# The down projection of a one-core encoder layer: a new order of its work, of its queues and of its sums

## The chip, the cores and the metric

The kernel runs on one core of one Trainium2 chip, as one launch. The metric is the device time of that launch in microseconds (us), and less is better. The core has five engines with a program each: TensorE (PE in the profile, its weight loads PEld), VectorE (DVE), ScalarE (ACT), GpSimd (POOL) and SyncE (SP), which only starts transfers. Sixteen DMA engines move data between the device's memory (DRAM) and the core's on-chip memory (SBUF). Transfers started by SP go through the hardware queue, those started by GpSimd through the software queue. TensorE writes its products to PSUM, a small memory of banks that VectorE and ScalarE read.

## What is computed

One layer of an encoder trunk, for 512 prompt frames and 64 frames of a running stream, in fp32. The change lies in its last part, the SwiGLU feed-forward block; x is the residual stream ahead of it.

```python
def rmsnorm(x, g):
    return x * lax.rsqrt(jnp.mean(x * x, axis=-1, keepdims=True) + EPS) * g

# ahead of this: norm, one input projection, stick-breaking attention on 8 heads, a gated short
# convolution on 8 channel groups, norm, output projection, residual
h2 = rmsnorm(x, g_norm2)                                        # (576, 2048)
x = x + (jax.nn.silu(h2 @ w_gate) * (h2 @ w_up)) @ w_down       # 2048 -> 5632 -> 2048
```

## The kernel before, in words

**Layout.** All activations are held transposed: 128 channels on the partitions, frames along the free axis, the 576 frames in two halves of 288 (`HALVES`). The hidden width of 5632 is 22 pairs (`NFP`) of 128-channel blocks; the 2048 output channels are 8 output blocks (`DC`) of two 128-channel columns each.

**fp32 by three products.** A weight or a frame tile is split into a rounded high part and the rest (`split`, L216: a ScalarE cast at L217, a VectorE subtraction at L218). A product is then three matmuls of 128x128 by 128x288: high by high, low by high, high by low. `multiply` (L1065) issues them; their line in the profile is L1069.

**Seven products per unit.** The feed-forward block is computed by a scheme in the manner of Strassen and Winograd. The two columns of weights and the two halves of the hidden pair and of the frames make 2x2 blocks, and seven products p = 1 to 7 take the place of eight. They need sums of weight blocks (L1055 to L1059, on VectorE: `s1`, `a21`, `a11`, and `a12` for p = 3) and sums of frame blocks, called forms: seven of them, each in a high and a low part. A unit is one entry of the list `UNITS`: 42 gate and up units, one per hidden pair 1 to 21 and per matrix (pair 0 is done ahead by `wide`, L972), and then the down visits. The products of neighbouring units are interleaved: (n+1,1), (n,3), (n,4), (n+1,2), (n+1,6), (n+1,7), (n+1,5). `prepare` (L1045) makes the sums and splits the weights of a product `AHEAD` = 2 products before `run` (L1073) multiplies. Accumulators in PSUM are shared between products: `psy` collects products 1, 6, 5 and 3 of a unit, `psw` products 7 and 4; ScalarE copies a state of `psy` that is needed later to SBUF (`kept`, L1079; tile `part`, one buffer per tag).

**Down visits.** The table `DOWN` (L44) has one entry (block, first pair, last pair) per visit: a visit multiplies the frames of its m pairs by that block's weights. There are 36 visits with m from 3 to 7. All 8 blocks must have gone past a pair before its storage is free for another (`down_calls`, L53).

**Frames.** At the end of gate and up, `put_form` (L922) stores each form to `hid_dram` from GpSimd's queue, 288 KB each. `load_pair` (L1148) reads one pair, seven forms in both parts, back as one load of 2016 KB from GpSimd's queue (L1152) into one of `SLOTS` = 7 slots. Pairs 0 to 2 are loaded during the last up unit, into storage of the activations `h2`; 3 at the first down visit, 4 to 6 at the next three, into storage of the frame sums (`tsum`, L896); the others when a slot comes free (L1217 on).

**Weights.** `load_weight` (L177, issue at L180) loads one 128-channel column of a unit from SP's queue, one load per column, two units ahead, into a buffer of 8 KB per partition, of which there are four.

**Residual and output.** `load_x2` (L1124) reads the residual x (`x2_dram`, written at L867) in 144 KB pieces from GpSimd's queue, 4 per block, and `add` (L1144) adds each result of a visit to it on VectorE, 7 additions a visit: four from PSUM, three from `part`. After the last visit of a block, `store_y` (L1154) waits three ticks (a tick is issued behind every pair of a product), transposes each 128x288 result on TensorE (L1173), copies it to a single output buffer `ob` on VectorE and ScalarE (L1174, L1176), and stores it from GpSimd's queue (L1163 to L1178).

**What sets the order.** TensorE's program is in the order in which the code is written, by hand, throughout (`manual_schedule`, L110). The other engines' programs are ordered by the language's own scheduler, except in an early stage (L360). Every DMA that SP starts takes one of eight lanes in turn and waits until the transfer eight before it on its queue is done.

## Time and profile before

| | us |
|---|---|
| median of the three runs | 2516.56 (2516.19 to 2518.26) |
| profiled execution, its own time | 2514.56 |
| span of that execution | 2512.9 |
| TensorE busy | 2427.3 (97%) |
| VectorE busy | 1759.8 (70%) |
| ScalarE busy | 1073.3 (43%) |
| GpSimd busy | 284.8 (11%) |
| mean granted TensorE clock | 0.988 of full speed |
| traffic | 269.33 MB read, 64.31 MB written |

The page of the profile gives busy time per engine, the span in 40 slices, DMA queues, the chain of work that ended last, and groups of instructions. A group reads: line, engine, operation, output tile <- input tiles, shapes, xcount, then busy time, mean ns of one, and the idle time of the engine just ahead of these instructions with the one that ended most of it. The table of stretches gives, per stretch of time, the busy us and the count of each engine, the granted clock, the share of the DMA engines that was busy and GB/s. In the table of waits a line reads: waiting instruction <- the one it waited for: total us, count, mean us. The list in order of time reads: start, length, engine, line, operation, and in brackets the idle time ahead of it and what ended it.

### The profile page before, as it was taken

The numbers are of one execution on the slowest core, as the hardware profiler recorded it, in microseconds if no ns is written. First come the engines' busy times: TensorE is split into PE (matmuls) and PEld (weight loads), VectorE is DVE, ScalarE is ACT, GpSimd is POOL, SyncE is SP. The second block draws the span as 40 slices with busy tenths as digits, with TensorE's granted clock in tenths as the row PEclk, the third lists the DMA queues.
The fourth block names the chain that finished last, engine by engine and source line by source line (L and its number), as shares of the span: only waits on it lengthen the run. The fifth ranks groups of instructions, "written<-read, shape, count | busy, mean of one in ns | idle before, by whom it ended". The sixth has DMA issues, their size and how long they took to land.

```text
span 2512.9 us, 44035 instructions
## 1 busy us (share of the span) xinstructions
PE 2427.3 (97%) x18137; PEld 2414.1 (96%) x18137; DVE 1759.8 (70%) x2772; ACT 1073.3 (43%) x1879; POOL 284.8 (11%) x515
## 2 busy tenths in 40 slices
PE   8999999999999999999999999999998798999887
PEld 8999999999999999999999999999998798999787
DVE  7666666363335458888888888888886687878665
ACT  6655555231132345444444444444443343444332
POOL 2101011110020120010010000101002100000133
PEclk9999999999999999999999999999999899999999
DMA  8322332222242343444444544434446635656532
GB/s 265 90 82 86 90 95 77 75 78 85 85 160 84 103 146 101 134 150 151 139 140 123 158 144 143 144 119 153 143 144 234 225 110 194 216 171 209 159 93 59
DMA packets 434177, 336.49 MB, mean 134 GB/s; under 512 B 10110, under 2 KB 411896, under 8 KB 431160
## 3 DMA queue, kind: packets, MB, share of 16 engines
q1 hardware_dynamic: 413624, 233.39, 32.1%
q0 software_dynamic: 20352, 100.29, 10.5%
q8 instruction: 142, 2.33, 0.4%
q14 instruction: 59, 0.48, 0.1%
HBM read 269.33 MB, written 64.31 MB: 133 GB/s over the span
## 4 chain that ended last, share of the span: by engine, by line
PE 87%; DMA 5%; DVE 3%; issue 2%; POOL 1%; ACT 1%; SPq 0%; POOLq 0%; DVEq 0%; ACTq 0%
PE psy L1069 29%; PE pj L209 23%; PE psw L1069 14%; PE pjo L209 8%; PE psx L1069 7%; DMA raw<-in_w_down_dram 3%; PE pw L984 2%; DMA out_dram<-ob 2%; POOL out_dram L1163 1%; DVE xlo L343 1%; PE z L547 1%; DVE whl L218 1%; PE po L613 1%; DMA hid_dram<-form 0%; POOL out_dram L1165 0%
## 5 line engine op out<-in xcount | busy, mean ns | idle before, releaser
L218 DVE TENSOR_TENSOR whl<-raw,whl 128x1024 fp32r<-128x1024 f32 (+5 forms) x468 | 481.6, 1029 | 89.9 <-ACT whl L217 88.3
L217 ACT CAST whl<-raw 128x1024 fp32r<-128x1024 f32 (+5 forms) x468 | 419.2, 897 | 278.7 <-issue 111.3
L209 PE MATMUL pj<-xhi,whi 128*128 128x288 f32 x1504 | 450.0, 299 | 0.1
L209 PE MATMUL pj<-xlo,whi 128*128 128x288 f32 x1504 | 444.5, 296 | 2.6 <-DVE xlo L343 2.6
L209 PE MATMUL pj<-xhi,wlo 128*128 128x288 f32 x1504 | 443.9, 295 | 0.3 <-DVE wlo L173 0.3
L1069 PE MATMUL psy<-slot,whl 128*128 128x288 f32 x2112 | 305.4, 301 | 44.3 <-DVE whl L218 21.4
L1069 PEld LDWEIGHTS psy<-slot,whl 128*128 128x128 f32 x2112 | 292.5, 193 | 46.2 <-DVE whl L218 21.9
L209 PEld LDWEIGHTS pj<-xlo,whi 128*128 128x128 f32 x1504 | 283.6, 189 | 3.4 <-DVE xlo L343 3.3
L209 PEld LDWEIGHTS pj<-xhi,wlo 128*128 128x128 f32 x1504 | 284.0, 189 | 0.8 <-DVE wlo L173 0.5
L209 PEld LDWEIGHTS pj<-xhi,whi 128*128 128x128 f32 x1504 | 283.9, 189 | 0.8 <-ACT whi L172 0.5
L1069 PE MATMUL psy<-tsum,whl 128*128 128x288 f32 x2016 | 281.1, 295 | 1.2 <-DVE whl L218 1.2
L1069 PE MATMUL psw<-tsum,whl 128*128 128x288 f32 x2016 | 280.9, 295 | 0.0
L1069 PEld LDWEIGHTS psy<-tsum,whl 128*128 128x128 f32 x2016 | 272.1, 189 | 1.5 <-DVE whl L218 1.5
L1069 PEld LDWEIGHTS psw<-tsum,whl 128*128 128x128 f32 x2016 | 271.8, 189 | 0.0
L1069 PE MATMUL psy<-h,whl 128*128 128x288 f32 x1764 | 248.8, 296 | 0.5 <-ACT part L1079 0.5
L1069 PEld LDWEIGHTS psy<-h,whl 128*128 128x128 f32 x1764 | 239.8, 189 | 0.7 <-ACT part L1079 0.7
L172 ACT CAST whi<-raw 128x1024 fp32r<-128x1024 f32 (+1 forms) x138 | 140.0, 1031 | 232.0 <-PE pj L209 95.8
L1079 ACT COPY part<-psy 128x288 f32<-128x288 f32 x234 | 93.2, 398 | 301.8 <-PE psy L1069 298.5
L926 POOL DMA_DIRECT2D hid_dram<-form x154 | 83.3, 541 | 895.4 <-DVE form L218 742.1
L173 DVE TENSOR_TENSOR wlo<-raw,whi 128x1024 fp32r<-128x1024 f32 (+1 forms) x132 | 160.2, 1226 | 23.8 <-ACT whi L172 21.9
L1069 PE MATMUL psw<-slot,whl 128*128 128x288 f32 x1056 | 154.6, 296 | 0.0
L1069 PEld LDWEIGHTS psw<-slot,whl 128*128 128x128 f32 x1056 | 145.5, 190 | 0.1
(338 smaller groups left out, 3759.5 us busy)
## 6 DMA issues: line engine op xcount, KB each, us to landing
raw<-in_w_in_dram SPq DMA_DIRECT2D x47, 1024.0 KB, 5.5
raw<-in_w_gate_dram SPq DMA_DIRECT2D x44, 1024.0 KB, 5.7
raw<-in_w_up_dram SPq DMA_DIRECT2D x44, 1024.0 KB, 6.0
hid_dram<-form POOLq DMA_DIRECT2D x154, 288.0 KB, 2.6
slot<-hid_dram POOLq DMA_DIRECT2D x22, 2016.0 KB, 9.8
raw<-in_w_down_dram SPq DMA_DIRECT2D x30, 640.0 KB, 4.6
raw<-in_w_out_dram SPq DMA_DIRECT2D x16, 1024.0 KB, 5.4
raw<-in_w_down_dram SPq DMA_DIRECT2D x12, 896.0 KB, 5.7
```

Source lines behind the costliest of these rows:

```text
L172: nc.scalar.copy(out=hi[:, a:b], in_=raw[:, a:b])
L173: lo_eng.tensor_tensor(out=lo[:, a:b], in0=raw[:, a:b], in1=hi[:, a:b].bitcast(F32), op=ALU.subtract)
L209: mm(ps, w_[:, k, csl], x_[:, k, a:b], start=(k == 0 and n == 0), stop=(k == nk - 1 and n == 2))
L217: nc.scalar.copy(out=hi, in_=src)
L218: (lo_eng or nc.vector).tensor_tensor(out=lo, in0=src, in1=hi.bitcast(F32), op=ALU.subtract)
L343: nc.vector.scalar_tensor_tensor(out=xlo[:, kt, :], in0=st, scalar=g1c[:, kt : kt + 1], in1=xhi[:, kt, :].bitcast(F32), op0=ALU.mult, op1= ...
L547: mm(zb[i], a_[:, kk], b_[:, q0:TP], start=(n == 0), stop=False, skip_group_check=True)
L613: mm(po[:, i * P : 512], a_[:, i, :], b_[:, : 512 - i * P], stop=(i == 0 and n == 2), **kw)
L926: nc.gpsimd.dma_start(out=hid_dram[fp][:, n - 1], in_=t.bitcast(F32))
L984: mm(pss[j, i], w_[:, k, j * P : (j + 1) * P], x_, start=(kk == 0 and k == 0 and n == 0), stop=(kk == 1 and k == 7 and n == 2))
L1069: mm(ps, whl[:, w_, j, :], x_, start=(start and j == 0 and q == 0), stop=(j == len(xs_) - 1 and q == 2), skip_group_check=True)
L1079: nc.scalar.copy(out=t, in_=st["y"])
```

## The change

It touches the feed-forward block from the first gate unit on, and most of it the down phase.

- **Program order.** From the first product of the last up unit on, ScalarE, VectorE, SP and GpSimd also run in the order in which the code is written, and `AHEAD` is 3.
- **Visits.** The table `DOWN` is another: 39 visits instead of 36, 11 of them of 3 pairs. The last two up units exchange the places of some products.
- **Frames.** `hid_dram` is laid out form by form, so that a partition's piece in it is 1152 bytes long instead of 16,128. Pairs are loaded by SP, not GpSimd. The slots lie in storage of `h2` (three of them) and of the frame sums (four of them): these are now in two parts, `t12` and `t34`. Pairs in slots 3 and 6 go as seven loads of 288 KB, since their storage is scattered. The first seven pairs are issued at the products of the last up unit (`turned`) at which their storage has been read for the last time.
- **Weights.** Four raw buffers of 8 KB per partition in two tiles are handed out by a free list (`load_columns`, `room`). A down unit of up to 4 pairs takes one buffer, a longer one two neighbouring ones, and both columns come in one load, so that a piece is 1 KB long instead of 512 bytes. The load is issued when the buffers are free, that is, after the last `prepare` that read them.
- **Sums.** A block's first visit writes its sums: ScalarE copies or VectorE adds two operands. In later visits VectorE adds what lies in PSUM and GpSimd adds what lies in `part`. An early addition stands right behind the product that ends it (p = 6, 7).
- **Residual.** It is no longer loaded ahead of the first visit; four accumulating transfers per block, started by GpSimd (`add_residual`), add it to the sums in SBUF later, between two visits of the block with at least four units between.
- **Output.** Transposed results go back into the storage of the sum itself, and the last 32 frames of a half into one of two buffers `obs`; the stores are started by SP, five ticks after the copies; the transposes come four ticks after the last sum instead of three.

The core of the diff:

```diff
 DOWN = (
-    (0, 0, 3), (1, 0, 4), (2, 0, 4), (3, 0, 4), (4, 0, 5), (0, 3, 7), (5, 0, 4), (6, 0, 5), (7, 0, 6),
-    (1, 4, 7), (2, 4, 8), (3, 4, 8), (4, 5, 10), (5, 4, 9), (6, 5, 10), (0, 7, 12), (7, 6, 11), (1, 7, 12),
-    (5, 9, 14), (2, 8, 15), (3, 8, 15), (4, 10, 15), (6, 10, 15), (7, 11, 16), (0, 12, 17), (1, 12, 15),
-    (5, 14, 19), (1, 15, 19), (2, 15, 22), (1, 19, 22), (3, 15, 22), (4, 15, 22), (5, 19, 22), (6, 15, 22),
-    (0, 17, 22), (7, 16, 22),
+    (0, 0, 3), (1, 0, 4), (2, 0, 4), (3, 0, 4), (0, 3, 7), (4, 0, 4), (5, 0, 4), (6, 0, 4), (7, 0, 7), (1, 4, 7),
+    (2, 4, 7), (3, 4, 8), (4, 4, 9), (5, 4, 9), (6, 4, 9), (0, 7, 10), (1, 7, 11), (2, 7, 12), (7, 7, 11), (3, 8, 13),
+    (4, 9, 15), (0, 10, 15), (5, 9, 16), (6, 9, 16), (1, 11, 16), (7, 11, 16), (2, 12, 17), (3, 13, 18), (1, 16, 19),
+    (5, 16, 19), (6, 16, 19), (0, 15, 22), (4, 15, 22), (2, 17, 22), (1, 19, 22), (5, 19, 22), (6, 19, 22), (3, 18, 22),
+    (7, 16, 22),
...
-    hid_dram = tc.dram_tile([NFP, P, FORMS, 2, HALF], F32, name="hid_dram")
+    hid_dram = tc.dram_tile([NFP, 2 * FORMS, P, HALF], F32, name="hid_dram")
...
+    t12 = tpool.tile([P, 2, NP - 1, 2, HALF], F32R, name="t12")
+    t12z = tpool.tile([P, 2, 2, HALF], F32R, tag="t12z", name="t12z")
+    t34 = []
+    def frame_sum(p_, j, f):
+        q = {5: 0, 6: 1, 7: 0, 4: 1}[p_]
+        return t34[j][:, q, f, :] if p_ in (7, 4) else t12[:, q, j, f, :] if j < NP - 1 else t12z[:, q, f, :]
...
-        nc.gpsimd.dma_start(out=hid_dram[fp][:, n - 1], in_=t.bitcast(F32))
+        nc.gpsimd.dma_start(out=hid_dram[fp][2 * n - 2 : 2 * n].rearrange("f p t -> p f t"), in_=t.bitcast(F32))
...
+    region = {}
+    free = []
+    wanted = [(0, 0), (1, 0), (0, 1), (1, 1)] + [(n, c) for n in range(2, NGU) for c in range(2)]
+    wanted += [(n, None) for n in range(NGU, len(UNITS))]
+    def room(n, c):
+        if c is not None:
+            return [h for h in free if h == ("AB"[c], n % 2)]
+        if UNITS[n][3] <= 4:
+            lone = [h for h in free if (h[0], 1 - h[1]) not in free]
+            return (lone or free)[:1]
+        both = [[(t, 0), (t, 1)] for t in "AB" if (t, 0) in free and (t, 1) in free]
+        return both[0] if both else []
+    def load_columns(gone=()):
+        free.extend(gone)
+        while wanted and room(*wanted[0]):
+            n, c = wanted.pop(0)
+            kind, i, a, m = UNITS[n]
+            w = {"gate": w_gate, "up": w_up, "down": w_down}[kind]
+            halves = room(n, c)
+            for h in halves:
+                free.remove(h)
+            t = raw_tile[halves[0][0]]
+            t = t[:, halves[0][1], :] if len(halves) == 1 else t.rearrange("p h e -> p (h e)")
+            wide_ = P if c is not None else 2 * P
+            c0 = 2 * i * P + (c or 0) * P
+            t = t[:, : 2 * m * wide_]
+            nc.sync.dma_start(out=t.rearrange("p (k e) -> p k e", e=wide_),
+                              in_=w[2 * a * P : 2 * (a + m) * P, c0 : c0 + wide_].rearrange("(k p) c -> p k c", p=P))
+            if c is None:
+                v = t.rearrange("p (j s h c) -> p j s h c", s=2, h=2, c=P)
+                region[n, 0], region[n, 1] = (v[:, :, :, 0, :], halves), (v[:, :, :, 1, :], ())
+            else:
+                region[n, c] = t.rearrange("p (j s c) -> p j s c", s=2, c=P), halves
...
+        if n == NGU - 2:
+            order += [(n + 1, 1), (n + 1, 2), (n, 3), (n + 1, 6), (n + 1, 7), (n + 1, 5), (n, 4)]
+            continue
...
+    def weight_sums(n, st):
+        m = UNITS[n][3]
+        st["a21"], st["a22"] = (region[n, 1][0][:, :, q, :] for q in range(2))
+        st["s1"] = w2pool.tile([P, NP, P], F32, tag="s1", name="s1")[:, :m]
+        nc.vector.tensor_tensor(out=st["s1"], in0=st["a21"], in1=st["a22"], op=ALU.add)
+        nc.vector.tensor_tensor(out=st["a21"], in0=st["a21"], in1=st["a11"], op=ALU.subtract)
+        nc.vector.tensor_tensor(out=st["a11"], in0=st["s1"], in1=st["a11"], op=ALU.subtract)
     def prepare(n, p_):
         st = unit.setdefault(n, {})
         m = UNITS[n][3]
         if p_ == 1:
-            st["a11"], st["a12"] = column(first_block + 2 * n, m)
+            st["a11"], st["a12"] = (region[n, 0][0][:, :, q, :] for q in range(2))
         src = {1: "a11", 2: "a12", 3: "a12", 4: "a22", 5: "s1", 6: "a11", 7: "a21"}[p_]
-        if p_ == 6:
-            st["a21"], st["a22"] = column(first_block + 2 * n + 1, m)
-            st["s1"] = w2pool.tile([P, NP, P], F32, tag="s1", name="s1")[:, :m]
-            nc.vector.tensor_tensor(out=st["s1"], in0=st["a21"], in1=st["a22"], op=ALU.add)
-            nc.vector.tensor_tensor(out=st["a21"], in0=st["a21"], in1=st["a11"], op=ALU.subtract)
-            nc.vector.tensor_tensor(out=st["a11"], in0=st["s1"], in1=st["a11"], op=ALU.subtract)
+        if p_ == 6 and n < NGU:
+            weight_sums(n, st)
         if p_ == 3:
             nc.vector.tensor_tensor(out=st["a12"], in0=st["a12"], in1=st["a11"], op=ALU.subtract)
         slot_turn[0] += 1
         whl = wpool.tile([P, 2, NP, P], F32R, tag=("whi", "wlo")[slot_turn[0] % 2], name="whl")[:, :, :m]
         split(whl[:, 0], whl[:, 1], st[src])
         operand[n, p_] = whl
+        if p_ == 2 and n >= NGU:
+            weight_sums(n, st)
+        if p_ in (3, 4):
+            st["gone"] = st.get("gone", 0) + 1
+            if n < NGU:
+                load_columns(region.pop((n, p_ - 3))[1])
+            elif st["gone"] == 2:
+                load_columns(region.pop((n, 0))[1])
...
-            add(n, c, i, ps)
+                finish(kind, fp, c, i, ps, part)
+            elif n in last:
+                store_y(n, c, i)
+        def add(c, i, ps, part=None):
+            if kind != "down":
+                return
+            if n in first:
+                if part is not None:
+                    nc.vector.tensor_tensor(out=acc[fp, c, i], in0=ps, in1=part, op=ALU.add)
+                else:
+                    nc.scalar.copy(out=acc[fp, c, i], in_=ps)
+                return
+            if ps is not None:
+                nc.vector.tensor_tensor(out=acc[fp, c, i], in0=ps, in1=acc[fp, c, i], op=ALU.add)
             if part is not None:
-                add(n, c, i, part)
-            if n in last:
-                store_y(n, c, i)
+                nc.gpsimd.tensor_tensor(out=acc[fp, c, i], in0=acc[fp, c, i], in1=part, op=ALU.add)
+        if kind == "down" and p_ == 1 and n in first:
+            take_blocks(fp)
+        later = n not in first
...
+    visits = {d: [n for n in range(NGU, NU) if UNITS[n][1] == d] for d in range(DC)}
+    first, last = {v[0] for v in visits.values()}, {v[-1] for v in visits.values()}
+    residual = {}
+    for d, v in visits.items():
+        n = next(a for a, b in zip(v, v[1:]) if a >= NGU + 10 and b >= a + 4)
+        residual.setdefault(n + 1, []).append(d)
...
+    def add_residual(d):
+        for c in range(2):
+            for i, (a, b) in enumerate(HALVES):
+                nc.gpsimd.dma_start(out=acc[d, c, i], in_=x2_dram[2 * d + c][:, a:b], accum_op=ALU.add)
...
     def load_pair(p):
-        tag = f"s{p % SLOTS}"
-        pool = h2pool if p % SLOTS < 3 else down["pool"]
-        slots[p] = pool.tile([P, FORMS, 2, HALF], F32R, tag=tag, name=f"slot{p}")
-        nc.gpsimd.dma_start(out=slots[p].bitcast(F32), in_=hid_dram[p])
+        q = p % SLOTS
+        if q in (3, 6):
+            slots[p] = [t34[f][:, q // 6] for f in range(FORMS)]
+            for f in range(FORMS):
+                nc.sync.dma_start(out=slots[p][f].bitcast(F32),
+                                  in_=hid_dram[p][2 * f : 2 * f + 2].rearrange("f p t -> p f t"))
+            return
+        if q in (2, 4):
+            t = t12[:, 1 - q // 4].rearrange("p j f t -> p (j f) t")
+        else:
+            t = h2s[q // 5][:, SB * (q % 5) : SB * (q % 5 + 1), :]
+        slots[p] = [t[:, 2 * f : 2 * f + 2, :] for f in range(FORMS)]
+        nc.sync.dma_start(out=t.bitcast(F32), in_=hid_dram[p].rearrange("f p t -> p f t"))
...
         def work():
-            yield 3
-            ob = down["pool"].tile([P, 3, P], F32, tag="ob", name="ob")
+            yield 4
             po = misc("pot")[:, : 3 * P]
             for q in range(3):
                 w = min(P, HALF - q * P)
                 nc.tensor.transpose(po[:w, q * P : (q + 1) * P], src[:, q * P : q * P + w], ident)
-            nc.vector.tensor_copy(out=ob[:, :2], in_=po[:, : 2 * P].rearrange("p (i c) -> p i c", c=P))
-            r = HALF - 2 * P
-            nc.scalar.copy(out=ob[:r, 2], in_=po[:r, 2 * P :])
+            ob = src[:, : 2 * P].rearrange("p (i c) -> p i c", c=P)
+            nc.vector.tensor_copy(out=ob, in_=po[:, : 2 * P].rearrange("p (i c) -> p i c", c=P))
+            obs = down["pool"].tile([r, P], F32, tag="obs", name="obs", bufs=2)
+            nc.scalar.copy(out=obs, in_=po[:r, 2 * P :])
+            yield 5
             if i == 0:
-                nc.gpsimd.dma_start(out=yp[: 2 * P, cs].rearrange("(i p) c -> p i c", p=P), in_=ob[:, :2])
+                nc.sync.dma_start(out=yp[: 2 * P, cs].rearrange("(i p) c -> p i c", p=P), in_=ob)
             else:
-                put(f0, ob[:, 0])
-                put(f0 + P, ob[:, 1])
-            put(f0 + 2 * P, ob[:r, 2])
+                put(f0, ob[:, 0, :])
+                put(f0 + P, ob[:, 1, :])
+            put(f0 + 2 * P, obs)
...
-    AHEAD = 2
+    turned = {(NGU - 1, 2): (0, 1), (NGU - 1, 6): (2,), (NGU - 1, 7): (3,), (NGU - 1, 5): (4,),
+              (NGU - 1, 3): (5,), (NGU - 1, 4): (6,)}
+    mode = ExitStack()
+    AHEAD = 3
     for k_ in range(AHEAD):
         prepare(*order[k_])
     for k_, (n, p_) in enumerate(order):
-        if p_ == 1:
-            for i in range(first_block + 2 * n, min(first_block + 2 * n + 4, len(specs))):
-                if i not in raws:
-                    load_weight(i)
-        if (n, p_) == (NGU, 1):
-            tpool.release()
-            ypool.release()
-            down["pool"] = tc.alloc_tile_pool(name="dpool", bufs=1, reuse_waits="tile", side="right")
-            load_pair(3)
-            load_x2(1)
-        if NGU < n < NGU + SLOTS - 3 and p_ == 1:
-            load_pair(n - NGU + 3)
+        if (n, p_) == (NGU - 1, 1):
+            mode.enter_context(tc.manual_schedule(engines={mybir.EngineType.Activation, mybir.EngineType.DVE,
+                                                           mybir.EngineType.SP, mybir.EngineType.Pool}))
+            down["pool"] = tc.alloc_tile_pool(name="dpool", bufs=1, reuse_waits="tile", side="left")
         if k_ + AHEAD < len(order):
             prepare(*order[k_ + AHEAD])
         run(n, p_)
-        if n == NGU - 1:
-            for p in {2: (0, 1), 3: (2,)}.get(p_, ()):
-                load_pair(p)
-            if p_ == 3:
-                load_x2(0)
-        if n >= NGU and p_ == 4:
-            new = [d for d, _, _ in DOWN[: n - NGU + 3] if (d, 0, 0) not in xt2]
-            for d in new:
-                load_x2(d)
-            for p in calls[n - NGU]:
-                load_pair(p)
+        for p in turned.get((n, p_), calls[n - NGU] if n >= NGU and p_ == 4 else ()):
+            load_pair(p)
+        if p_ == 2:
+            for d in residual.get(n, ()):
+                add_residual(d)
...
```

133 lines of the change are left out of this document (64 added, 69 removed).

## The prediction, made before the change had run

> **What bounds the kernel now.** I read the page first, then the table of stretches, then the instructions in order of time at the holes, then the waits of the tail and the groups of the Vector engine.
>
> ```profile
> span 2512.9 us, 44035 instructions
> PE 2427.3 (97%) x18137; PEld 2414.1 (96%) x18137; DVE 1759.8 (70%) x2772; ACT 1073.3 (43%) x1879; POOL 284.8 (11%) x515
> ```
>
> TensorE is the bound, and nearly all its idle time lies in the down phase, which starts at 1926.4. Columns of the stretches: stretch, length, busy time and count of PE, PEld, DVE, ACT, POOL, granted clock, DMA share, GB/s.
>
> ```profile
> 1926.40:1976.00 49.60, 23.36 (x136) 22.66 (x135) 18.85 (x39) 10.80 (x23) 19.90 (x37) 0.72 0.92 338
> 1976.00:2068.00 92.00, 92.00 (x681) 92.00 (x680) 77.95 (x133) 40.49 (x73) 0.00 (x0) 0.98 0.36 101
> 2068.00:2100.00 32.00, 21.18 (x144) 20.70 (x143) 15.93 (x32) 8.79 (x18) 2.12 (x4) 0.84 0.75 292
> 2100.00:2320.00 220.00, 220.00 (x1666) 220.00 (x1665) 183.30 (x286) 94.94 (x157) 5.30 (x10) 1.00 0.57 180
> 2320.00:2350.00 30.00, 23.20 (x165) 22.97 (x164) 18.70 (x28) 10.66 (x17) 0.53 (x1) 0.89 0.67 242
> 2350.00:2512.90 162.90, 136.08 (x1013) 131.46 (x1011) 102.95 (x171) 53.29 (x106) 53.43 (x96) 0.98 0.31 86
> ```
>
> The fourth row is the pace with nothing late: 220/1666 = 0.132 us per matmul, clock 1.00, DVE busy 83%. At that pace the other rows lose 49.6-136x0.132 = 31.6, 2.1, 13.0, 8.2 and, up to the last matmul at 2503.9, 20.2 us; half-speed matmuls behind each hole (clock 0.72 to 0.89) are in these. From 2503.9 to the end is a drain of 9.0. The phase has 8x22x7x3 = 3696 product matmuls and 96 transposes: 3792x0.132 = 500.7, so undisturbed it would end at 1926.4+500.7 = 2427.1.
>
> Why the holes: at 2084.7 PE stops while ScalarE waits for weights. Four pair loads of 2 MB stand on the software queue, in packets of 16,128 bytes; the weights come in packets of 512 bytes.
>
> ```profile
> 2084.73 0.30 PE L1069 MATMUL psw<-slot,whl 128*128 128x288 f32 x1
> 2093.95 0.62 ACT L217 CAST whl<-raw 128x512 fp32r<-128x512 f32 x1 [13.01 <-DMA raw<-in_w_down_dram]
> 2094.92 2.29 PE L1069 MATMUL psy<-slot,whl 128*128 128x288 f32 x8 [9.89 <-ACT part L1079]
> ```
> ```profile
> slot<-hid_dram POOLq DMA_DIRECT2D x4, 2016.0 KB, 15.4
> raw<-in_w_down_dram SPq DMA_DIRECT2D x3, 640.0 KB, 6.3
> ```
>
> A packet occupies its engine for 601 ns (16,128 B), 93 (2304), 46 (1024) or 27 (512; medians of the trace). Queues that take turns packet by packet leave the weights 27 ns of every 628. The hole at 1958-1973 (14.6 us) is the same with seven pairs and 32 residual blocks. In the tail the one output buffer is what is late:
>
> ```profile
> ACT ob L1176 <- DVE ob L1174: 54.4, 24, 5.0
> DVE ob L1174 <- DMA out_dram<-ob: 30.2, 15, 3.9
> PE pot L1173 <- DVE x L1146: 15.7, 11, 2.8
> ```
>
> **The change, part by part.** A visit is one entry of DOWN, with m pairs; it has 7 products of 3m matmuls (0.396m us). Time before 1926.4: the waits of the weight loads stand at the same instructions as before up to the output projection, and gate/up runs at 100% PE; a load there is still freed two units ahead (22 us for a 5.7 us load). 0 us, bounds -2 to +3.
>
> *Start.* Pairs load as their storage comes free in the last up unit: 0 and 1 at 1926.4-7x3.17 = 1904.2, 2 at 1910.6, then 3, 4, 5, 6. In one queue order counts. A pair is 14x128 packets of 1152 B, by interpolation between 46 and 93 ns 51 ns each: 1792x51/16 = 5.7 us; 4 pairs of weights are 1024 packets of 1 KB: 2.9. 0, 1, weights 1, 2 need 20 us from 1906: landed 1927 to 1928; visit 0 uses pair 2 from 1927.2. Form stores (7x288 KB, about 5 us of the engines) push it to 1930 to 1932: 3 to 4 us lost. Pair 3 follows about 9 us later, used at 1936; the seventh pair, 1955 to 1960, is needed at 1970. The forms have two buffers: ScalarE, in program order, waits for a form store (landing 2.6 median, 7.2 in the crowd) before it casts weights for the 1.2 us products of visit 0: 3 to 5. With a slow clock behind it, 9 instead of 33.7; bounds 3 and 18.
>
> *Visit 8 to 12.* Visit 8 frees pairs 7-10: 4x5.7 = 23 us of queue from its end, 106.8 us into the phase. The weights of visit 12 (5 pairs, 3.7 us) stand behind them: landed 106.8+23+3.7+2.2 = 135.7. Its first product is due at 130.1, 5/7 through visit 11. 5.6 late, about 1.5 of cast and subtract, 2 of slow clock: 9 instead of 13.0; bounds 4 and 20. What is late is now weights behind frames in the same queue, no longer beside them. Elsewhere a burst is at most three pairs (17 us), and the next large load is due 20 us or more later; visit 31 (5.2 us of weights behind 20 and 21) is within 1. 1 instead of 8.2; bounds 0 and 8.
>
> *Sums.* Before, 36x7 = 252 adds on DVE; after, 8x3+31x4 = 148, 8 ScalarE copies (0.40), 93 GpSimd adds. 39 visits instead of 36 add 33 weight passes of 0.15 fixed, 5 us. The row:
>
> ```profile
> L1146 DVE TENSOR_TENSOR x<-part,x 128x288 f32<-128x288 f32 x40 | 18.2, 455 | 8.0 <-ACT part L1079 7.6
> ```
> 104x0.455 = 47 us less DVE work. But GpSimd work costs DVE:
>
> ```profile
> L857 DVE SCALAR_TENSOR_TENSOR h<-x,vec,h x21: 505/519/1074, 833.2 to 920.1; 128x288 fp32r<-128x288 f32 x21
> L864 POOL TENSOR_TENSOR acc<-acc,sq x30: 798/806/1084, 839.8 to 932.6; 128x288 f32<-128x288 f32 x30
> ```
> Where such an add overlaps, DVE needs 1.07 instead of 0.52. 93x0.55 = 51: DVE gains nothing, about 457 of 501 us, and stands under PE except on 3-pair visits: 11x0.555+4x0.455+3x0.55 = 9.5 against 8.3. The three-product lead (3.6 us) covers two in a row; three (28-30) show. 4 us, bounds 0 and 15. The Trainium skill, SBUF — State Buffer, "Who interferes with whom", says that a VectorE instruction with two SBUF inputs and a GpSimd one that reads SBUF exclude each other for a whole instruction. By it the cost could be 93x0.81 = 75 and DVE 481, the sum 5 to 8 us more; the row shows a part of one instruction lost, which I take.
>
> *Residual.* 32 plain loads become 32 accumulating ones, issued at least two visits before the sum's next use: 0.54 each on POOL by the same shape before (0.536), 2 at most. Hidden by over 20 us; if POOL were held 8 us, the single part buffers would stop ScalarE: 0, bounds -1 (the 32 loads leave the first crowd, counted above) and 12.
>
> *Queues.* SP gains 58 pair loads and 96 output stores, 0.43 each; 8 loads may be open. A store waits 5 ticks behind its copies, so the weights behind it wait under 1 us; POOL loses 118 issues.
>
> *Tail.* No output buffer to wait for. New: transposes wait for PE end, DVE add 0.46, GpSimd add 0.81 and hand-overs, 1.55 us, against 4 ticks = 1.59; each DVE backlog shows. Half the 32 blocks at 0.4, plus the 3-pair visits 34-36: 12 instead of 20.2; bounds 4 and 25. Drain without the 3.8 us wait for the buffer: 5.5 instead of 9.0.
>
> *Small transfers.* Six pairs go as seven loads of 288 KB. The nearest row is 16 loads of 288 KB, issued 0.43 apart and landed after 6.1 each: they overlap. 0; bounds 0 and 75 (a rival).
>
> **Sum.** 2427.1+9+9+1+4+12+5.5 = 2467.6 span; the profiled execution is 2514.56 for 2512.9, so 2469.3. The median of the runs, 2516.56, is 2.0 above that execution: 2471.
>
> **Rivals.**
> - *Queue-bound.* If 1152-byte packets run at 250 GB/s (before: 292 to 338 in crowded stretches), a pair takes 8.2: +8 at the start, +10 at visit 12, 3 to 5 each at visits 18, 26 and 31: 2471+32 = 2503. For it: one queue, everything behind everything. Against: 46 ns packets are 356 GB/s.
> - *Near the floor.* Forms hidden, visit 12 late by 5, tail 4: 2446. For it: the fourth stretch holds PE at 100% for 220 us.
> - *Slower: program order.* If cast, subtract, copy and add of a product run one after another instead of three products ahead, a 4-pair product takes 0.62+0.69+0.40+0.455 = 2.17 against 1.59, a 3-pair one 1.92 against 1.19. On the 21 visits with m up to 4 that is 77x0.58+70x0.73 = 96 us: 2567. It decides once 47% of these products are hit. Against: DVE at 83% costs PE nothing now with two products ahead.
> - *Small loads one by one.* If those seven loads did not overlap, at the 2.6 us of a 288 KB form store they would take 18.2 instead of 5.7, and six such pairs up to 75: 2546. Against: the row of 16 overlapping loads. The Trainium skill, DMA: Bandwidth & Descriptors, "Rules for kernel authors", wants 1 MiB or more per transfer, and its fit of 2.0 us plus bytes/436 GB/s would make such a pair about 19 us.
> - *Nothing changes.* The slots come free at the same products; if arrival, not order, were the limit, 2515.
>
> **How the numbers follow.** Forecast 0.50, own range 2455 to 2488; queue-bound 0.18; near the floor 0.15; program order 0.11; small loads 0.02; nothing changes 0.04. The range 2444 to 2512 leaves out half of the low case and the last three. 0.2% (5 us) is what a measurement of this kernel can tell: faster 0.84, same 0.03, slower 0.13.
>
> **What would show it.** Right: frames on the hardware queue in 1152-byte packets; a hole of 5 to 10 us near 2060 that ends with visit 12's weights; none of 14 us at the start; DVE rows of 128x384 above 0.56 beside GpSimd adds; no wait for an output buffer. Wrong: clock under 0.95 in the middle stretch, or casts there that wait for a copy (program order); many weight waits (queue-bound); ScalarE waiting for GpSimd (residual).

## The result and the profile after

The changed kernel takes 2503.77 us in the median of four runs (2501.98 to 2507.3), against 2517.0 before: a ratio of 0.9949, interval 0.9931 to 0.9966. It is faster by about 13 us where 46 were forecast. The profiled execution took 2507.3 us, for the span shown here; these are the page's first lines of the changed kernel:

```profile
span 2505.6 us, 44203 instructions
PE 2442.1 (97%) x18137; PEld 2425.9 (97%) x18137; DVE 1752.2 (70%) x2701; ACT 1075.8 (43%) x1917; POOL 348.1 (14%) x490
```

The down phase begins at 1935.7. The next view is the table of stretches of the changed kernel (columns as before), cut at the start, visit 12, visit 18, visits 31 to 33 and the tail:

```profile
1935.70:1977.50 41.80, 29.26 (x203) 28.79 (x202) 24.93 (x46) 15.66 (x34) 3.64 (x5) 0.84 0.96 330
...
2070.80:2100.50 29.70, 22.61 (x153) 21.93 (x152) 19.49 (x29) 10.00 (x19) 8.98 (x10) 0.89 0.80 235
...
2162.00:2187.60 25.60, 22.30 (x153) 21.59 (x152) 17.41 (x26) 9.34 (x18) 10.22 (x13) 0.93 0.59 151
...
2338.80:2385.10 46.30, 40.29 (x273) 38.98 (x272) 32.65 (x47) 16.58 (x30) 9.38 (x9) 0.93 0.40 129
...
2399.50:2501.10 101.60, 89.17 (x644) 84.26 (x643) 66.82 (x118) 35.51 (x87) 16.54 (x19) 0.98 0.30 86
```

The stretches are cut at the same matmuls in every kernel below: 200, 150, 150, 270 and 642 of them (the x of a row also counts those that reach in from outside). At the forecast's 0.132 us each, a stretch's length less its matmuls is its loss. The start loses 41.8-26.4 = 15.4, visit 12 loses 9.8, visit 18 5.8, visits 31 to 33 10.6, and the tail 16.8. Everything between them loses 6.3 together. About half of that is no hole: between the start and visit 12 TensorE is never idle, and its 700 matmuls take 93.3 us, 133.3 ns each instead of 132. Over the 2380 matmuls between the named places that makes 3.2 us.

What stands behind the holes is in the list of instructions in order of time:

```profile
1942.52 0.43 ACT L211 CAST form<-ut 128x288 fp32r<-128x288 f32 x1 [5.53 <-DMA hid_dram<-form]
1942.85 0.51 ACT L211 CAST whl<-raw_a 128x384 fp32r<-128x384 f32 x1
...
1950.03 0.43 ACT L211 CAST form<-ux 128x288 fp32r<-128x288 f32 x1 [4.22 <-DMA hid_dram<-form]
...
1951.22 1.81 PE L1112 MATMUL psy<-h_s,whl 128*128 128x288 f32 x6 [12.19 <-ACT part L1122]
...
2087.23 0.72 ACT L211 CAST whl<-raw_b 128x640 fp32r<-128x640 f32 x1 [8.05 <-DMA raw_b<-in_w_down_dram]
...
2453.01 0.26 ACT L1261 COPY obs<-pot 32x128 f32<-32x128 f32 x1 [5.41 <-DMA out_dram<-obs]
```

At the start ScalarE stands twice at the cast of a form, because its buffer's store has not landed (5.53 and 4.22 us), and the cast of weights that TensorE needs stands behind it in program order. At 2087 the weights of visit 12 are late, as forecast. In the tail ScalarE stands 5.41 us at a copy into `obs` for an output store, again with casts behind it.

### The profile page after: what moved, and what is told of

It reads as the page before. It is cut to its first block, busy times and chain, and to the rows that moved or that the text cites. A ratio compares the mean times of both kernels' runs of the same rounds, so it can differ in the third digit from the quotient of the medians.

```text
span 2505.6 us, 44203 instructions
## 1 busy us (share of the span) xinstructions
PE 2442.1 (97%) x18137; PEld 2425.9 (97%) x18137; DVE 1752.2 (70%) x2701; ACT 1075.8 (43%) x1917; POOL 348.1 (14%) x490
## 5 line engine op out<-in xcount | busy, mean ns | idle before, releaser
L1112 PE MATMUL psy<-t,whl 128*128 128x288 f32 x2916 | 445.4, 298 | 11.4 <-ACT part L1122 9.6
L1112 PE MATMUL psy<-h_s,whl 128*128 128x288 f32 x2724 | 419.4, 298 | 16.4 <-ACT part L1122 15.7
L1112 PEld LDWEIGHTS psy<-t,whl 128*128 128x128 f32 x2916 | 410.0, 191 | 14.2 <-ACT part L1122 10.8
L1112 PEld LDWEIGHTS psy<-h_s,whl 128*128 128x128 f32 x2724 | 383.6, 191 | 18.8 <-ACT part L1122 17.0
L1112 PE MATMUL psw<-t,whl 128*128 128x288 f32 x2592 | 380.9, 297 | 0.0
L212 DVE TENSOR_TENSOR whl<-raw_a,whl 128x1024 fp32r<-128x1024 f32 (+5 forms) x288 | 303.0, 1052 | 83.2 <-ACT whl L211 81.9
L1112 PEld LDWEIGHTS psw<-t,whl 128*128 128x128 f32 x2592 | 358.8, 190 | 0.0
L211 ACT CAST whl<-raw_a 128x1024 fp32r<-128x1024 f32 (+5 forms) x288 | 255.3, 894 | 142.4 <-DVE raw_a L1082 50.2
L212 DVE TENSOR_TENSOR whl<-raw_b,whl 128x1024 fp32r<-128x1024 f32 (+5 forms) x198 | 195.2, 987 | 96.1 <-ACT whl L211 94.9
L1112 PE MATMUL psx<-h_s,whl 128*128 128x288 f32 x1122 | 168.8, 299 | 6.0 <-DVE gs L961 6.0
## 6 DMA issues: line engine op xcount, KB each, us to landing
h_s<-hid_dram SPq DMA_DIRECT2D x10, 2016.0 KB, 12.6
```

The source lines that it names most:

```text
L211: nc.scalar.copy(out=hi, in_=src)
L212: (lo_eng or nc.vector).tensor_tensor(out=lo, in0=src, in1=hi.bitcast(F32), op=ALU.subtract)
L1112: mm(ps, whl[:, w_, j, :], x_, start=(start and j == 0 and q == 0), stop=(j == len(xs_) - 1 and q == 2), skip_group_check=True)
```

## The experiments

Each run is compared with the kernel before, measured beside it. All losses are in us and come from the profile of the run, cut as above.

| kernel | median | ratio, interval | start | visit 12 | visit 18 | 31 to 33 | tail |
|---|---|---|---|---|---|---|---|
| changed | 2503.8 | 0.9949 (0.9931 to 0.9966) | 15.4 | 9.8 | 5.8 | 10.6 | 16.8 |
| third form buffer | 2493.2 | 0.9907 (0.9889 to 0.9925) | 9.3 | 10.0 | 4.5 | 10.8 | 17.1 |
| residual early | 2506.6 | 0.9956 (0.9941 to 0.9970) | 14.8 | 12.6 | 0.3 | 9.0 | 18.7 |
| 4-pair visits at 29, 30 | 2493.3 | 0.9897 (0.9879 to 0.9915) | 15.3 | 9.6 | 5.0 | 4.6 | 12.7 |
| visit 12 of 4 pairs | 2496.7 | 0.9920 (0.9903 to 0.9937) | 14.6 | 1.7 | 4.2 | 9.9 | 16.7 |
| residual spread | 2501.5 | 0.9935 (0.9920 to 0.9950) | 15.4 | 9.3 | 0.3 | 10.7 | 18.5 |
| five `obs` | 2498.4 | 0.9924 (0.9909 to 0.9939) | 14.8 | 9.4 | 5.9 | 10.3 | 13.2 |
| part added on VectorE | 2508.0 | 0.9961 (0.9946 to 0.9976) | 14.6 | 12.5 | 7.9 | 7.6 | 18.5 |
| no program order | 2468.2 | 0.9802 (0.9786 to 0.9818) | 7.9 | 4.6 | 0.0 | 6.0 | 1.6 |
| order on ScalarE, VectorE | 2492.3 | 0.9897 (0.9881 to 0.9913) | 14.6 | 5.5 | 0.3 | 10.6 | 13.8 |
| order on SP, GpSimd | 2482.2 | 0.9854 (0.9834 to 0.9874) | 7.7 | 10.8 | 5.6 | 6.8 | 7.3 |
| order on ScalarE | 2479.3 | 0.9846 (0.9825 to 0.9867) | 14.2 | 6.7 | 0.2 | 5.3 | 4.7 |
| order on VectorE | 2482.4 | 0.9866 (0.9851 to 0.9880) | 15.5 | 3.6 | 0.3 | 9.7 | 5.9 |
| lead of 2, program order | 2524.9 | 1.0032 (1.0021 to 1.0042) | 16.8 | 12.3 | 3.3 | 11.0 | 20.5 |
| lead of 2, no order | 2466.2 | 0.9801 (0.9786 to 0.9815) | 7.2 | 3.4 | 1.3 | 6.7 | 1.0 |
| five mends, program order | 2478.0 | 0.9844 (0.9830 to 0.9859) | 9.0 | 1.5 | 0.2 | 5.2 | 13.5 |
| five mends, later copies | 2476.4 | 0.9840 (0.9825 to 0.9854) | 9.7 | 1.5 | 0.2 | 5.0 | 13.9 |
| five mends, `obs` by VectorE | 2467.5 | 0.9800 (0.9779 to 0.9821) | 10.0 | 1.5 | 0.2 | 6.7 | 9.0 |
| five mends, no order | 2453.0 | 0.9742 (0.9725 to 0.9759) | 4.2 | 0.2 | 0.2 | 4.9 | 1.4 |

### Four holes, one edit each

**A third form buffer.** The storage of `ax`, idle until block 3, takes every third form.

```diff
-        t = tmp.tile([P, 2, HALF], F32R, tag="hl", name="form")
+        turn_f[0] += 1
+        if "pool" in down and turn_f[0] % 3 == 0:
+            t = down["pool"].tile([P, 2, HALF], F32R, tag="ax", name="form3")
+        else:
+            t = tmp.tile([P, 2, HALF], F32R, tag="hl", name="form")
```

> Every third form is staged in the storage of ax, so that forms have three buffers instead of two. Theory (two buffers and slow form stores stop ScalarE at the start): ScalarE's waits for form stores between 1935 and 1952 (5.5 and 4.2 us) go to under 1 us; the start row, which lost 15.0 us, loses 5 to 9, since by bytes (four pairs, three weight loads and seven forms, 13.1 MB at 356 GB/s from 1911.7) pair 3 lands near 1948 and is wanted near 1942. 6 to 10 us off the median of 2503.8: 2494 to 2498. Rival (the pairs' arrival is the limit): a hole of about 12 us stays and ends with a frame load: 2502 to 2506.

The start loses 9.3 instead of 15.4, at the edge of what was expected. The rest is not the arrival of pair 3: TensorE's hole of 6.0 us still ends with ScalarE, which waits 3.67 us for one more form store. So the mechanism stands, and three buffers are too few. Of the median's 10.6 us only some 6 are the hole. What the others are is not shown; the last section tells what sets this profile apart.

**The residual early.**

```diff
-        n = next(a for a, b in zip(v, v[1:]) if a >= NGU + 10 and b >= a + 4)
-        residual.setdefault(n + 1, []).append(d)
+        n = NGU + {0: 6, 1: 4, 2: 5, 3: 5, 4: 7, 5: 8, 6: 9, 7: 12}[d]
+        residual.setdefault(n, []).append(d)
```

> The residual transfers are started at visits 4 to 9 and 12, where the queues are nearly empty, instead of from visit 11 on. Theory (accumulating transfers take queue time from the frames and weights of visit 18): the traffic in the crowd near 2150 stays near 356 GB/s instead of 245, the loss near 2166 goes from 6.6 us to under 1.5: 2497 to 2499. Rival (SP's eight lanes with seven small loads hold the weights): the loss stays above 5 us: 2502 to 2506.

Near visit 18 the loss went from 5.8 to 0.3, so the residual was its cause and not SP's lanes. But the time did not fall: 6.1 us more were lost before visit 12 and 2.8 at it, because the weights of the 7-pair visit 8 now stood beside the residual. What such a transfer costs is in the view of DMA traffic: packets, MB and share of sixteen engines for each queue. The changed kernel from 2130 to 2170 us:

```profile
q1 hardware_dynamic: 7856, 8.55, 65.2%
q0 software_dynamic: 1873, 1.92, 31.7%
```

The kernel with the residual early, from 1997 to 2023 us:

```profile
q0 software_dynamic: 2729, 2.80, 82.5%
```

On the average a packet of the plain loads took 0.652x16x40/7856 = 53 ns of an engine, one of the residual's queue 0.317x16x40/1873 = 108 ns. These counts include some packets of 4 bytes and, among the plain ones, weights in packets of 1024 bytes. The packets of 1152 bytes alone took 52 and 111 ns (medians of the same 40 us). Nearly alone, the residual filled 82.5% of the engines at 109 GB/s. Its 4096 packets take 28 us of all sixteen.

**The residual spread.** Same edit, with `{0: 24, 1: 4, 2: 5, 3: 6, 4: 22, 5: 25, 6: 26, 7: 28}`.

> The residual transfers again, one block at a time: blocks 1, 2, 3 at visits 4, 5, 6, and 4, 0, 5, 6, 7 at visits 22, 24, 25, 26, 28, where one or no pair is in flight. Theory (an accumulating packet takes 111 ns of a queue engine against 53 for a plain one of 1152 bytes, so a block of 512 packets takes about 3.6 us of all sixteen; it costs TensorE only where weights or frames are already tight): the loss near visit 18 is under 1.5 us as in the kernel with all of them moved early, and no new loss above 2 us appears: 2496 to 2500. Rival (28 us of queue time show wherever they are put): 3 us or more are lost at another visit, and the time is 2502 to 2507.

The loss at visit 18 is 0.3 again and none of 3 us appears elsewhere (0.8 more ahead of visit 12, 1.7 more in the tail); the time of 2501.5 lies between the theory's range and the rival's. The place of these transfers is worth 5.5 us in that hole. The 2 us in the median are less than the two intervals can tell apart.

**4-pair visits at 29 and 30.**

```diff
-    (5, 16, 19), (6, 16, 19), (0, 15, 22), (4, 15, 22), (2, 17, 22), (1, 19, 22), (5, 19, 22), (6, 19, 22), (3, 18, 22),
+    (0, 15, 19), (4, 15, 19), (5, 16, 22), (6, 16, 22), (2, 17, 22), (0, 19, 22), (3, 18, 22), (4, 19, 22), (1, 19, 22),
```

> From visit 28 on the table is another: (1,16,19), (0,15,19), (4,15,19), (5,16,22), (6,16,22), (2,17,22), (0,19,22), (3,18,22), (4,19,22), (1,19,22), (7,16,22); as many visits and products as before. Theory (weights of a 7-pair visit wait for two neighbouring buffers, which 3-pair visits free only some 10 us ahead): the 11.5 us lost from 2345 to 2395 go to 2 to 4, the tail stays within 3 of its 16: 2494 to 2498. Rival (the queue behind pairs 20 and 21 is the limit): a loss of 8 us or more stays there: 2500 to 2505.

Visits 31 to 33 lose 4.6 instead of 10.6, and the tail 4 less. In the changed kernel the weights of visit 31 were issued at 2345.91, after the DMA engines had stood idle, and their cast waited 4.0 us: no queue was late, the load itself was, since a 7-pair visit waits for two neighbouring buffers. TensorE's two long waits there are 3.0 us behind this cast and 2.6 at a transpose that waits for an addition of GpSimd; a wait of the second kind, 2.2 us, stays in the kernel with 4-pair visits.

**Visit 12 of four pairs.**

```diff
-    (2, 4, 7), (3, 4, 8), (4, 4, 9), ...
-    (4, 9, 15), ...
+    (2, 4, 7), (3, 4, 8), (4, 4, 8), ...
+    (4, 8, 15), ...
```

> Visit 12 takes pairs 4 to 7 instead of 4 to 8, and visit 20 takes pair 8 with its own, so that the weights of visit 12 fit one buffer and are issued ahead of pairs 7 to 10. Theory (weights behind four pairs in one queue): the hole near 2082 (9.5 us with the slow clock) goes to under 2, nothing takes its place: 2494 to 2497. Rival (frames or a weight buffer of the 5-pair visits are late as well): 5 us or more are lost at visit 12 or 13, ended by frames or by the weights of visit 13: 2500 to 2505.

The hole went from 9.8 to 1.7, and what follows up to visit 18 lost 3.2 more. The weights were late because they were issued behind the four pairs.

**Five output buffers.** `bufs=2` becomes `bufs=5` for `obs`.

> Five buffers obs instead of two. Theory (the last 32 frames' copy waits for its buffer's store, 5.4 us once, and stops ScalarE's casts in program order): the hole of 4.4 us in the tail goes, the tail's loss falls from 16.8 to 10 to 12: 2497 to 2500. Rival (the transposes' wait for VectorE's last sums is the cause): the hole stays, ended by a VectorE sum, and the tail loses 15 or more: 2501 to 2506.

TensorE's hole behind that wait (4.1 us in the trace, called 4.4 above) went, and with it 3.6 of the tail's 16.8. The tail still loses more than the 10 to 12 expected. The other 13.2 have another cause.

### Whose order costs

**No program order.** All that is left out is the order; everything else is the changed kernel.

```diff
-            mode.enter_context(tc.manual_schedule(engines={mybir.EngineType.Activation, mybir.EngineType.DVE,
-                                                           mybir.EngineType.SP, mybir.EngineType.Pool}))
```

> The down phase without program order on ScalarE, VectorE, SP and GpSimd; their programs are ordered by the language's scheduler as before, all else as in the changed kernel. Theory (program order keeps a form's cast, which waits for its buffer's store, ahead of the casts of weights): the start loses 9 or less instead of 15, the middle stretch is the same, so 2494 to 2500. Rival (program order is what keeps weights and loads early): losses of more than 10 us in the middle or the tail, 2510 to 2540.

The theory was right in direction and far too small. The time is 2468.2, 35.5 us below the changed kernel. The page and the table of stretches of this kernel, cut at the same matmuls:

```profile
span 2466.1 us, 44181 instructions
PE 2429.9 (99%) x18137; PEld 2418.5 (98%) x18137; DVE 1764.6 (72%) x2701; ACT 1079.3 (44%) x1917; POOL 354.5 (14%) x490
```
```profile
1933.40:1967.70 34.30, 29.61 (x203) 29.15 (x202) 24.65 (x46) 15.35 (x33) 3.63 (x5) 0.90 1.08 371
...
2061.00:2085.40 24.40, 21.99 (x153) 21.54 (x152) 20.19 (x30) 9.74 (x18) 11.91 (x15) 0.93 0.88 234
...
2145.70:2165.50 19.80, 19.80 (x152) 19.80 (x152) 17.05 (x23) 8.65 (x16) 7.86 (x8) 1.00 0.42 100
...
2320.00:2361.60 41.60, 37.99 (x271) 37.29 (x271) 35.20 (x48) 17.24 (x31) 9.04 (x9) 0.96 0.40 127
...
2375.00:2461.40 86.40, 84.66 (x645) 83.09 (x643) 65.69 (x116) 36.80 (x87) 18.56 (x19) 1.00 0.34 102
```

The tail takes 86.4 us for the matmuls that took 101.6, with VectorE, ScalarE and GpSimd as busy as there (65.7, 36.8 and 18.6 against 66.8, 35.5 and 16.5). So no engine was short of time in the tail; it was the order that cost it. TensorE's longest waits there are at the transposes (`pot`), for VectorE's last sums, first of the changed kernel, then without program order:

```profile
PE pot L1257 <- DVE acc L1142: 8.4, 6, 4.1
PE pot L1257 <- DVE acc_z L1142: 2.2, 1, 2.2
```
```profile
PE pot L1257 <- DVE acc L1142: 0.6, 1, 0.6
```

ScalarE's waits in the tail, in the same order, show what stands ahead of the casts:

```profile
ACT obs L1261 <- DVE acc L1259: 27.4, 18, 3.2
ACT obs L1261 <- issue: 11.2, 4, 4.4
ACT obs L1261 <- DMA out_dram<-obs: 6.8, 2, 5.4
```
```profile
ACT part L1122 <- PE psy L1112: 17.6, 16, 3.5
ACT obs L1261 <- DVE acc L1259: 11.0, 8, 3.3
```

45 us of waits at `obs` become 12, and ScalarE mostly waits for TensorE, as an engine that is ahead does. Visit 18 loses nothing here although the residual is the same: the scheduler starts its transfers one by one behind their own sums, from 2061 on, where program order starts them in fours, three blocks of them between 2143 and 2171; and it starts five of pair 13's seven small loads at 2106, where program order has them at 2142.

**Two engines at a time.** The set of engines in that statement is `{Activation, DVE}`, or `{SP, Pool}`.

> Program order on ScalarE and VectorE alone; SP and GpSimd are ordered by the language's scheduler. Theory (a cast or copy that waits, for a form's buffer, an output buffer or a late load, holds the casts written behind it): the time stays near that with all four in program order, 2495 to 2505, with 13 us or more lost at the start and in the tail each. Rival (it is SP's and GpSimd's order, so that loads are issued late): 2465 to 2476, near the 2468.2 of no program order.

> Program order on SP and GpSimd alone; ScalarE and VectorE are ordered by the scheduler. Theory (as before: ScalarE's and VectorE's order is what costs): 2465 to 2476, the tail loses under 4 us and the start under 10. Rival (SP's and GpSimd's order costs): 2490 to 2505.

Neither time lies in a range that was named: 2492.3 and 2482.2 are both between theory and rival, so both pairs of engines cost time. Against 2468.2, ScalarE's and VectorE's order costs 24.1 us, SP's and GpSimd's 14.0, and both 35.5. They cost it at different places. The start (14.6 against 7.7) and visits 31 to 33 (10.6 against 6.8) are ScalarE's and VectorE's; visit 18 (0.3 against 5.6) and most of visit 12 (5.5 against 10.8) are SP's and GpSimd's; the tail is both.

**One engine.** `{Activation}`, and `{DVE}`.

> Program order on ScalarE alone. Theory (ScalarE carries the cost: form casts and obs copies that wait hold the casts of weights): 12 us or more are lost at the start, 8 or more in the tail, 2482 to 2494. Rival (VectorE's order carries it): 2464 to 2474.

> Program order on VectorE alone. Theory (ScalarE carries the cost): 2464 to 2474. Rival (VectorE's order carries it, its sums and copies hold the low parts of weights): 2480 to 2494, with the loss in the tail above 8 us.

Neither carries it alone: 11.1 us for ScalarE's order and 14.2 for VectorE's. Either is enough to lose the start (14.2 and 15.5), since a form's high part stands on ScalarE and its low part on VectorE, each with weights behind it. In the tail each loses 4.7 and 5.9, and both 13.8: the two together lose more than both losses added. That fits two engines that wait for each other; the run with `obs` by VectorE below tests a part of it.

**The lead.** `AHEAD = 2` in place of 3, in program order and without.

> The changed kernel with weights prepared two products ahead instead of three. Theory (in program order a wait is covered by the lead only): 3-pair visits and the tail lose 8 us or more beyond what they lost, 2511 to 2530. Rival (the lead is not what is short): 2500 to 2507.

> No program order, and weights prepared two products ahead. Theory (the scheduler moves work past a wait, so the lead matters little): within 6 us of 2468.2. Rival (the lead matters under any order): 2476 to 2490.

Both theories hold. In program order the third product of lead is worth 21 us, and without it the change would have made the kernel slower than before (1.0032). With the scheduler's order it is worth nothing that can be told apart (2466.2 against 2468.2).

### The sums, and all mends together

**Part added on VectorE.** `nc.gpsimd.tensor_tensor` of `part` becomes `nc.vector.tensor_tensor`.

> The additions of part stand on VectorE instead of GpSimd. Theory (GpSimd's additions slow VectorE by as much as they take from it): VectorE's busy time in the down phase stays within 10 us and the time within 4 of 2503.8. Rival (they relieve VectorE): VectorE is busier by 93 x 0.455 = 42 us, the visits of three pairs and the tail lose 5 us or more beyond what they lost: 2508 to 2516.

At 2508.0 the time is 4 us longer, at the edge of both ranges, and the two intervals overlap. VectorE's busy time from the first matmul of the down phase to the end goes from 410.0 to 417.7. 93 additions of 0.455 came to it, 42 us, so some 34 us came off its other work. The groups of VectorE between 1977 and 2339 show which, first with the additions on GpSimd, then on VectorE:

```profile
L212 DVE TENSOR_TENSOR whl<-raw_b,whl 128x640 fp32r<-128x640 f32 x42 | 38.0, 905 | 24.5 <-ACT whl L211 24.3
L212 DVE TENSOR_TENSOR whl<-raw_a,whl 128x640 fp32r<-128x640 f32 x18 | 17.8, 990 | 9.4 <-ACT whl L211 9.4
```
```profile
L212 DVE TENSOR_TENSOR whl<-raw_b,whl 128x640 fp32r<-128x640 f32 x42 | 34.5, 821 | 23.0 <-ACT whl L211 22.9
L212 DVE TENSOR_TENSOR whl<-raw_a,whl 128x640 fp32r<-128x640 f32 x18 | 14.8, 821 | 5.6 <-ACT whl L211 4.7 <-PE psw L1112 0.8
```

The same subtraction takes 905 or 990 ns beside GpSimd's additions and 821 without. On the average each of GpSimd's additions cost VectorE 0.37 us, so the change takes little off VectorE: in the down phase it was busy 417.7 us in the kernel before. Where the two meet, one waits for the other. In the changed kernel a subtraction that takes 0.82 alone took 2.60 beside two additions of 1.89 together, nearly the sum:

```profile
2106.31 2.60 DVE L212 TENSOR_TENSOR whl<-raw_a,whl 128x640 fp32r<-128x640 f32 x1 [0.73 <-ACT whl L211]
2106.33 1.89 POOL L1144 TENSOR_TENSOR acc<-acc,part 128x288 f32<-128x288 f32 x2
```

The additions are stretched as well: 0.80 us at the least, 0.98 in the median and up to 1.52 (the 69 into `acc`).

**Five mends.** Third form buffer, five `obs`, visit 12 of four pairs, 4-pair visits at 29 and 30, residual spread; in program order and without.

> The changed kernel, in program order, with five mends at once: a third form buffer, five obs, visit 12 of four pairs, 4-pair visits at 29 and 30, residual transfers spread. Theory (the holes are separate places, each with its own late thing): their gains add, 6 at the start, 8 at visit 12, 5.5 near visit 18, 7.5 at visits 31 to 33, 4 for obs, 31 in all: 2469 to 2477. Rival (each mend moves the loss to the next place): 2482 to 2495.

> The same five mends without program order. Theory (visit 12's weights behind four pairs, 4.6 us, and the buffers of visit 31, 5.6 us, are lost under any order; the rest is program order's): 2454 to 2461. Rival (the scheduler's order already gives what the mends give, or is upset by them): 2464 to 2474.

In program order 25.8 us come off where 31 were expected: each hole shrinks as it did alone, and the tail keeps 13.5. Without program order the same mends give 2453.0, 1 us below the expected range: 2.6% below the kernel before, and the fastest of all. They gain 15 us there, some 12 of them at places that the profile shows: 4.4 at visit 12, 3.7 at the start, 3.3 between the named places, but only 1.1 at visits 31 to 33, where 4.9 stay. Of these, 2.5 are one transpose that waits for an addition of GpSimd, as in the kernel with 4-pair visits alone.

**Later transposes and copies,** in the kernel with five mends and program order: `yield 4` becomes `yield 6`, and a `yield 3` stands between the transposes and their copies.

> The kernel with five mends in program order (2478.0), and in it the transposes of an output six ticks behind its last sum instead of four, and their copies three ticks behind the transposes. Theory (in program order the copies stand right behind the transposes, wait for them and for VectorE, and hold the casts; the transposes wait for sums): the tail's loss falls from 13.5 us to 6 or less, 2467 to 2473. Rival (VectorE has too much to do in the tail in any order): the tail loses 11 or more, 2476 to 2483.

The theory falls: the tail loses 13.9, so it is not the place of the copies, two or three ticks earlier or later, that loses it.

**`obs` by VectorE,** in the same kernel:

```diff
-            nc.scalar.copy(out=obs, in_=po[:r, 2 * P :])
+            nc.vector.tensor_copy(out=obs, in_=po[:r, 2 * P :])
```

> The kernel with five mends in program order (2478.0), with the copy of the last 32 frames on VectorE instead of ScalarE. Theory (ScalarE waits there for VectorE's copy, 42 us in all, while VectorE waits for ScalarE's casts): the tail's loss falls from 13.5 to 8 or less, 2468 to 2474. Rival (the transposes' wait for the sums is enough to lose it): 12 or more, 2475 to 2482.

The tail loses 9.0, between the two bounds: a third of it was ScalarE's wait for VectorE's copy. Of the other 9.0 the trace shows the place: TensorE's transposes still wait 5.8 us, for last sums on VectorE (5.2) and GpSimd (0.6). Why these sums come late in program order was not found. The median fell by 10.5 us, 6 more than the tail's gain; the two profiled executions differ by 4.5, as the tail does, and the four runs of this kernel lie 10 us apart.

## Why the prediction was wrong

The direction was right, the size was not. The step that failed is the price of program order: the sum gave it 3 to 5 us at the start and no term anywhere else, and left the rest to a rival with a chance of 0.11. The runs show 35.5 us for it (2503.8 against 2468.2). That the kernel without program order lies where the forecast (2471) put the changed one is in part luck: its down phase begins 7.0 later than forecast, and its tail loses 10.4 less. Term by term:

| term | forecast | changed | no program order |
|---|---|---|---|
| down phase begins | 1926.4 | 1935.7 | 1933.4 |
| start | 9 | 15.4 | 7.9 |
| visit 12 | 9 | 9.8 | 4.6 |
| visit 18 (residual) | 0 | 5.8 | 0.0 |
| visits 31 to 33 | 1 | 10.6 | 6.0 |
| sums, and all between | 4 | 6.3 | 7.3 |
| tail | 12 | 16.8 | 1.6 |
| drain, from the last matmul's start | 5.5 | 4.6 | 4.8 |

- **Start.** The mechanism was named, ScalarE before a form store in program order, but priced at 3 to 5 us. The step had the time of a store in the crowd (6.0 here) but charged one wait; there were two, of 5.53 and 4.22, one behind the other, and TensorE stood 12.2.
- **Program order** was a rival with a chance of 0.11, in the wrong form. It asked whether one product's chain fits between products, and looked for a slow middle stretch; the middle ran at 100%. The cost is that one late thing, a form store, an output store or a load, holds all that is written behind it on its engine. A lead of three products covers 3.6 us on 3-pair visits, and the waits were 4 to 8.
- **Visit 12** was right in cause and size (9 against 9.8): weights behind four pairs in one queue. About half of it is the order of SP and GpSimd, which has the loads in that sequence (5.5 without their program order, 10.8 with it alone). A pair's rate was right too: 53 ns for a packet where 51 were interpolated, 355 GB/s in the crowd. That the measured 2503.8 equals the queue-bound rival's 2503 is chance: its premise, 250 GB/s for packets of 1152 bytes, did not come about; the traffic fell to 245 only for a few us near visit 18, beside the residual.
- **Residual.** Priced at 0 with bounds of -1 and 12, and 5.8 came. The sum priced its issue on GpSimd (0.85 us measured, 0.54 taken) and gave its packets no price of their own; they took 111 ns where plain ones took 52.
- **Visits 31 to 33.** Queue time was counted, and the lead of the free buffers was not: a 7-pair visit needs two neighbours, which 3-pair visits free late (the table has 10 visits of 3 pairs, not the 11 of the section on the change). A transpose's wait of 2.6 us for GpSimd had no term either.
- **Tail.** The place was named, the transposes behind the last sums. Two things that make them late were missed: two `obs` are an output buffer to wait for just as the one `ob` was (3.6 us), and the crossing waits of ScalarE and VectorE in program order. The sum charged VectorE's backlog; without program order, and with VectorE as busy, the tail lost 1.6, less than the low bound of 4.
- **Ahead of the phase** 9.4 us were lost where 0 was taken, with bounds of -2 and 3. At the start of the kernel, in code that is the same, the profiled executions lie up to 4 us apart, and this one had 3.0 more than the one before. The entry into the feed-forward block lost 3.2 more, some 1.4 to 3.1 of them by the lead of three: the first 200 matmuls there lose 8.7 to 10.3 with it in all the runs and 7.1 to 7.3 with a lead of two. The rest, 3.2, is the pace of the matmuls (below).
- **Sums.** GpSimd's additions give VectorE almost nothing, as forecast, at 34 us instead of 51. The Trainium skill, SBUF — State Buffer, "Who interferes with whom", has the two exclude each other for a whole instruction; the trace agrees where they meet (2.60 us for 0.82 and 1.89 above). The average of 0.37 is lower since many of the additions meet a part of a VectorE instruction or wait themselves. And the seven small loads of a pair overlapped: they landed after 6.3 us each in the row of 2325 to 2365, at 345 to 387 GB/s. The Trainium skill, DMA: Bandwidth & Descriptors, "Anatomy of one DMA — SWDGE (gpsimd) path", gives the fit of 2.0 us plus bytes/436 GB/s for one transfer started by GpSimd; seven times that, as the prediction's rival took it, is not what these loads on SP's queue show.

## What to carry to other kernels

Program order on an engine turns each wait on it into a wait of everything behind it: before fixing an order, list the instructions that can wait for a transfer or for a buffer's last store, and see that the lead covers the longest of them, or leave these engines to the scheduler. A free list of buffers has its own lead, counted in products between the last use and the first, and short visits ahead of long ones use it up. An accumulating transfer is not free because its issue is: count its packets at their own price.

## What the runs showed of the hardware

Two things were not expected. An accumulating packet of 1152 bytes took 111 ns of a DMA engine, a plain one 52 (medians from 2130 to 2170 us of the changed kernel).

And the pace of the matmuls differs between profiled executions at full clock and with TensorE never idle. Rows of the same stretch, of the kernel before, of the changed one, and of the one with a third form buffer:

```profile
1100.00:1500.00 400.00, 400.00 (x3013) 400.00 (x3012) 335.76 (x459) 185.11 (x279) 34.08 (x63) 1.00 0.46 141
```
```profile
1100.00:1500.00 400.00, 400.00 (x3003) 400.00 (x3002) 333.70 (x456) 183.25 (x277) 45.21 (x62) 1.00 0.47 141
```
```profile
1100.00:1500.00 400.00, 400.00 (x3028) 400.00 (x3027) 337.00 (x460) 184.59 (x279) 45.87 (x63) 1.00 0.47 142
```

132.8, 133.2 and 132.1 ns a matmul. The code of this stretch is the same in the last two kernels. All the other profiles of the changed kernel's variants show the pace of the second row, so the third is the exception. Over the 6800 matmuls of gate and up 1.1 ns make 7.5 us, most of the 10.2 by which the two down phases begin apart (1935.7 and 1925.5). There is one profile of each kernel, so it is not shown whether the execution or the kernel decides. In four kernels one of the four runs was 4 to 9 us faster than the other three (2469.7 beside 2479.0 to 2480.4 with order on ScalarE alone), which would fit the execution. So a profile places a stretch's own holes well, but two kernels' spans can differ by some 8 us for another reason than their holes. What sets the pace was not tried.
